# Two-layer hybrid block: attention's loads get an order of their own, other stages' weights are loaded ahead and split by GpSimd

## The chip, the cores and the metric

The kernel runs on one core of a Trainium2 chip. The metric is the device time of one execution in microseconds (us). The engines are TensorE (PE; its weight loads are listed apart as PEld), VectorE (DVE), ScalarE (ACT), GpSimd (POOL) and SyncE (SP), which in this kernel issues every transfer.

## The reference

The reference is a two-layer block with fp32 inputs and outputs: 1024 latent tokens (`x`) and 256 context tokens (`ctx`) of width 1024. Four mixers share one in-projection and one out-projection:

```
for l in range(2):
    sh, sc, gt = split(silu(c) @ w_mod[l] + b_mod[l], 3)       # the same from c_ctx for the context
    h  = rms_norm(x, g_pre[l]) * (1 + sc) + sh                 # latent and context
    p  = h @ w_in[l]
    a  = MLA attention, 4 heads (64 + 32 rotary), v 64         # softmax over 1024 + 256 keys
    g  = grouped-query attention, 4 heads, 2 key heads of 64   # the same keys' length
    s  = state-space mixer (two scans), finish: z = gelu(y + d*u); z * sigmoid(z @ glu_w + glu_b)
    y  = Hyena mixer (two long convolutions)
    x  = x + gt * rms_norm(concat[a, g, s, y] @ w_out[l], g_post[l])
```

The context is attended to and projected out in the first layer only. `a`, `g`, `s` and `y` are each multiplied by the silu of a part of `p`. `gt`, the gate, takes columns 2048 to 3071 of `w_mod`; `sh` and `sc` take the others.

## The kernel before

Everything is fp32. A large matmul takes three TensorE passes on operands split in two float32r parts, a rounded high one and the rest (names end in `h`/`hi` and `l`/`lo`); the split is a cast and a subtraction. Layer 0 runs from 0 to 1230 us, layer 1 from there to the end. In each layer come the mixers with the in-projection (`ipc`, operand `hh`, `hl`, weights `whi`, `wlo`), then attention, then the out-projection (`ops`).

**Attention** (`attention`, L1518 and below). The work is a list of units: for each pair of heads (g0, g1 of grouped-query attention, then m0, m1 of MLA), each block of 256 queries and each of the pair's two heads. Layer 0 has 40 units, layer 1 has 32, without the context's queries. A unit multiplies keys and queries for 1024 latent keys (`aS`) and 256 context keys (`acx`), takes the row maxima (`am`, DVE), the exponentials (`aP`, ACT), transposes them (`apt`), splits them (`aPh` on ACT, `aPl` on DVE) and multiplies by the values (`apo`). The sums' reciprocals are spread by GpSimd (`aLB`, L1665) and multiplied in. The string `ORDER` (L1515) writes the steps of neighbouring units out as one interleaved order, and a token (`keep`) makes the scheduler hold to it on every engine. Loads carry no token in this version: `load_q` asks for the queries `aq` three units ahead and, at a pair's first unit, for its keys `kst`, its values `vst` and, for m0, the rotary keys `krope`; the scheduler places them in SP's queue.

**Side work.** The last step of `ORDER`, `X`, calls `pump`, which advances a generator by one step a unit. In layer 0 it yields 24 steps of `mod_steps`: load 512 KB of `w_mod` (`mraw`), cast it on ACT (`mhi`, L326), subtract on GpSimd (`mlo`), multiply (`mps`, four matmuls a step), add to `msb`. Eight steps are this layer's gate, sixteen the next layer's shift and scale. Then, in both layers, 16 steps of `out_weights` load `w_out` (`owr`, 256 KB), cast it on ACT (`owh`, L1730) and subtract on GpSimd (`owl`). Layer 1's gate is not side work: `mod_plain` computes it right after the in-projection, ahead of attention, by 16 fp32 matmuls `mps<-wraw,csl`.

**The end of the mixers.** In layer 1 the last mixer work is `ssm_finish` (L1301): four chunks of 256 tokens, each with two loads `sgy`, `sgg` for each half, the gelu, which ends with `sz` on DVE, then `sglu` on PE, `sth` and a store to `mixD`. In layer 0 it is the Hyena mixer's context part, which ends with the stores `mixD<-hcz`.

**Order and queues.** The scheduler orders instructions by program order as far as their data and buffers allow. SP issues its transfers strictly in order and has eight semaphores, so a transfer also waits for the one eight before it to land. A buffer of a new pool that overlaps one of a closed pool waits for the last reader of that: `kst`, `vst` and `aq` of the first pair lie where the in-projection's operand was.

Of the kernel before, what the change touches and what calls it, by code (L numbers as in the profile page):

```python
# [11 lines left out]
F32 = mybir.dt.float32  # L12
# [175 lines left out]
class K:  # L188
# [114 lines left out]
    def mod_plain(self, l, blk):  # L303

        ps = self.f("mps")
        for k in range(8):
            raw = self.wp.tile([128, 512], F32, tag="wraw", name="wraw", bufs=2)
            self.load(raw, self.A["w_mod"][l, blk, :, k])
            self.mm(ps[:2], self.sc[:, k], raw, k == 0, k == 7)
        ms = self.wp.tile([4, 512], F32, tag="ipo", name="msb", bufs=3)  # L310
        self.nc.vector.memset(ms, 0.0)
        self.nc.scalar.copy(ms[:2], ps[:2])
        yield ms

    MODHI = "AA"

    def mod_steps(self, P, l, blk):
# [3 lines left out]
        for k in range(0, 8, 2):  # L321
            raw = P.tile([128, 2, 512], F32, tag="mraw", name="mraw", bufs=3)
            hi, lo = (P.tile([128, 2, 512], F32R, tag="m" + t, name="m" + t, bufs=2) for t in ("hi", "lo"))
            self.load(raw, self.A["w_mod"][l, blk, :, k:k + 2])
            for j, c in enumerate(self.MODHI):
                self.keep(nc.scalar.copy(hi[:, j], raw[:, j]) if c == "A" else (nc.gpsimd if c == "P" else nc.vector).tensor_copy(hi[:, j], raw[:, j]))  # L326
            self.lo(lo, raw, hi, nc.gpsimd)
            ps = self.f("mps")
# [36 lines left out]
    def mod_gates(self, l, steps):  # L365

        gD = self.mg = self.dram.tile([4, 1024], F32, name=f"modg{l}")
        for blk in range(2):
            for ms in steps(l, 4 + blk):
                if ms is not None:  # L370
                    self.store(gD[:, blk * 512:(blk + 1) * 512], ms)
                yield

    def mod_next(self, l, steps, P):

        *self.mod, put = self.mod_cols(l, P)
        for blk in range(4):
            for ms in steps(l, blk):
                if ms is not None:
                    put(blk, ms)  # L380
# [1137 lines left out]
    def attention(self, l, P, W, nq, side):  # L1518
# [18 lines left out]

        def keys(src):
# [435 lines left out]
```

## Time and profile before

| | us |
|---|---|
| median of 3 runs | 2233.22 (2231.14 to 2233.59) |
| profiled execution | 2229.03 |
| its span | 2226.9 |
| PE busy | 1956.9 (88%) |
| DVE busy | 1587.0 (71%) |
| ACT busy | 958.3 (43%) |
| POOL busy | 924.1 (41%) |
| chain that ended last | PE 43%, DVE 26%, DMA 12%, issue 6%, POOL 4%, ACT 4%, SPq 4% |

How to read it: the span is the first to the last instruction of the profiled execution. The chain follows the last instruction back to what released it, step by step; its DMA share is time in which the end of the kernel waited for a transfer, its SPq share for SP's queue. A timeline row gives start, length, engine, line, operation and tile, the number of instructions in a row, and in brackets idle time before it with its releaser. A windows row gives a stretch, its length, the busy time (and instructions) of PE, PEld, DVE, ACT and POOL (with a tile's name, those of its instructions, without the engines that have none), then the clock granted to TensorE (1.00 is 2.4 GHz), the busy share of the DMA engines and what they moved. A group row gives line, engine, operation, tiles, shape and count, then total busy us and mean ns, then idle time before and releasers. The trace can miss a few matmuls, so counts may be short by one or two.

### The profile page before, as it was taken

Reading aid. Unit: us, or ns where it says so; the run is one execution under the profiler, and the core shown is the slowest. Engines: PE = TensorE matmul, PEld = TensorE weight load, DVE = VectorE, ACT = ScalarE, POOL = GpSimd, SP = SyncE. Lnnn points to the kernel's source line nnn. Section 1 sums busy time; section 2 is a strip of 40 time slices with the busy share of each in tenths; the row PEclk is TensorE's granted clock in tenths of the full one; section 3 lists DMA queues with packets and bytes.
Section 4 is the critical chain, followed back from the end, with each engine's and each line's share of the span. In section 5 each row is a group of like instructions: output and inputs, shape, how many; then the busy total and the mean of one; then the engine's idle time right before and its main releaser. Section 6 shows DMA issues by size and latency. Waiting matters only on the chain.

```text
span 2226.9 us, 31563 instructions
## 1 busy us (share of the span) xinstructions
PE 1956.9 (88%) x10811; PEld 1624.3 (73%) x10811; DVE 1587.0 (71%) x2976; ACT 958.3 (43%) x2040; POOL 924.1 (41%) x726
## 2 busy tenths in 40 slices
PE   5797998889899689999799988987988968999888
PEld 2577887777778477778577776986766736899866
DVE  8799339856886479889444598399478836999822
ACT  4422233224333388777332322342232226987711
POOL 4656235664561133230156557247666602100034
PEclk8698899999999899999799987998999988999989
DMA  7323364337764845431343423363466577431063
GB/s 222 112 91 115 123 207 133 96 118 224 223 202 155 223 118 157 126 102 39 112 160 105 153 94 142 126 217 119 112 205 217 159 224 174 115 102 42 17 183 123
DMA packets 262402, 316.56 MB, mean 142 GB/s; under 512 B 46783, under 2 KB 203711, under 8 KB 258914
## 3 DMA queue, kind: packets, MB, share of 16 engines
q1 hardware_dynamic: 262242, 314.55, 46.4%
q8 instruction: 85, 1.39, 0.3%
q14 instruction: 75, 0.61, 0.1%
HBM read 207.61 MB, written 106.86 MB: 141 GB/s over the span
## 4 chain that ended last, share of the span: by engine, by line
PE 43%; DVE 26%; DMA 12%; issue 6%; POOL 4%; ACT 4%; SPq 4%; POOLq 0%; DVEq 0%; ACTq 0%
PE ipc L224 9%; PE ops L224 7%; PE apo L224 6%; PE apt L253 5%; PE aS L224 5%; SPq L201 4%; DVE sD L233 3%; DVE lU L233 2%; DMA px<-qkvD 2%; DVE sp L233 1%; PE acx L224 1%; PE lout L224 1%; ACT aPh L1637 1%; DMA krope<-mR 1%; PE hps L224 1%
## 5 line engine op out<-in xcount | busy, mean ns | idle before, releaser
L224 PE MATMUL ipc<-hh,whi 128*128 128x512 f32 (+2 forms) x992 | 386.8, 390 | 25.1 <-DVE ipt L236 10.1
L224 PE MATMUL ipc<-hl,whi 128*128 128x512 f32 (+2 forms) x992 | 380.6, 384 | 1.6 <-POOL hl L233 1.6
L224 PE MATMUL ipc<-hh,wlo 128*128 128x512 f32 (+2 forms) x992 | 381.7, 385 | 0.0
L233 DVE TENSOR_TENSOR aPl<-apt,aPh 128x512 fp32r<-128x512 f32 x328 | 224.8, 685 | 54.7 <-ACT aPh L1637 50.0
L224 PEld LDWEIGHTS ipc<-hh,whi 128*128 128x128 f32 x992 | 196.7, 198 | 60.9 <-DVE ipt L236 13.6
L233 POOL TENSOR_TENSOR wlo<-wraw,whi 128x512 fp32r<-128x512 f32 x108 | 158.8, 1475 | 147.1 <-ACT whi L443 145.7
L224 PEld LDWEIGHTS ipc<-hh,wlo 128*128 128x128 f32 x992 | 196.2, 198 | 32.4 <-issue 3.2
L1637 ACT CAST aPh<-apt 128x512 fp32r<-128x512 f32 x328 | 187.3, 592 | 71.5 <-PE apt L253 66.0
L224 PEld LDWEIGHTS ipc<-hl,whi 128*128 128x128 f32 x992 | 196.0, 198 | 30.1 <-POOL hl L233 2.3
L1665 POOL COPY aLB<-am 128x128 f32<-128x128 f32 x72 | 21.0, 292 | 419.5 <-DVE am L1657 419.5
L253 PE MATMUL apt<-ident,aP 128*128 128x128 f32 x1312 | 191.2, 276 | 2.5 <-DVE aPl L233 1.3
L1602 DVE TENSOR_REDUCE am<-aS 128x1 f32<-128x1024 f32 x128 | 155.8, 1217 | 33.6 <-PE aS L224 33.4
L224 PE MATMUL aS<-kst,aq 128*128 128x512 f32 x512 | 155.1, 426 | 21.7 <-DMA aq<-gP 12.2
L246 ACT ACTIVATE aP<-aS,am,rs 128x1024 f32<-128x1024 f32 x128 | 155.9, 1218 | 19.1 <-DVE am L243 17.4
L224 PE MATMUL apo<-aPh,vst 128*128 128x256 f32 x656 | 140.7, 312 | 23.7 <-ACT aPh L1637 18.6
L253 PEld LDWEIGHTS apt<-ident,aP 128*128 128x128 f32 x1312 | 150.3, 141 | 10.9 <-DVE aPl L233 5.5
L224 PE MATMUL apo<-aPl,vst 128*128 128x256 f32 x656 | 125.0, 288 | 3.4 <-DVE aPl L233 3.3
L224 PEld LDWEIGHTS apo<-aPh,vst 128*128 128x128 f32 x656 | 97.3, 192 | 39.1 <-ACT aPh L1637 24.7
L443 ACT CAST whi<-wraw 128x512 fp32r<-128x512 f32 x124 | 75.4, 618 | 99.0 <-PE ipc L224 52.4
L224 PEld LDWEIGHTS aS<-kst,aq 128*128 128x128 f32 x512 | 89.8, 196 | 36.6 <-issue 19.7
L224 PEld LDWEIGHTS apo<-aPl,vst 128*128 128x128 f32 x656 | 100.8, 191 | 11.4 <-DVE aPl L233 6.5
L224 PE MATMUL ops<-owh,omh 128*128 128x512 f32 x288 | 94.8, 410 | 15.7 <-ACT omh L1749 10.5
(372 smaller groups left out, 4469.6 us busy)
## 6 DMA issues: line engine op xcount, KB each, us to landing
wraw<-in_w_col_dram SPq DMA_DIRECT2D x64, 256.0 KB, 3.0
wraw<-in_w_mod_dram SPq DMA_DIRECT2D x48, 256.0 KB, 3.4
mraw<-in_w_mod_dram SPq DMA_DIRECT2D x24, 512.0 KB, 4.1
kst<-mK SPq DMA_DIRECT2D x16, 640.0 KB, 8.7
omx<-mixD SPq DMA_DIRECT2D x18, 512.0 KB
ogt<-gD SPq DMA_DIRECT2D x18, 512.0 KB, 4.3
k<-kt SPq DMA_DIRECT2D x16, 512.0 KB, 3.5
lk<-k SPq DMA_DIRECT2D x8, 1024.0 KB, 7.3
```

What stands on the lines that cost most here:

```text
L201: self.nc.sync.dma_start(out=out, in_=in_)
L224: self.keep(self.nc.tensor.matmul(out, lhsT, rhs, start=start, stop=stop))
L233: self.keep((eng or self.nc.vector).tensor_tensor(out=out, in0=a, in1=b, op=op))
L246: self.keep(self.nc.scalar.activation(out=out, in_=in_, func=func, **k))
L253: self.keep(self.nc.tensor.transpose(out, in_, self.ident[:p, :p]))
L443: self.nc.scalar.copy(hi, raw)
L1602: self.keep(nc.vector.tensor_reduce(out=x["m"][:, 2 + qi:3 + qi], in_=x["S"][qi], axis=AX.X, op=ALU.max))
L1637: self.keep(nc.scalar.copy(h, ps))
L1665: self.keep(nc.gpsimd.tensor_copy(x["LB"][:, :, o:o + 64], x["m"][:, 10:12].unsqueeze(2).to_broadcast([128, 2, 64])))
```

## The change

- `load` returns its instruction, and attention's own loads go through `fetch`, which stamps them with a second token: among themselves they keep the written order, and are not placed ahead of it.
- Attention takes three pools. The first pair's keys, values and all query buffers (`kst0`, `vst0`, `aq`) come from a pool above the in-projection's operand in memory, the later pairs' from another one.
- `feed` loads side work's weights ahead: `mraw` two steps ahead in three buffers, `owr` three ahead in four (two buffers before).
- The cast of `w_mod` and `w_out` to the high part moves from ACT to GpSimd, which does the subtraction as before: a 128x1024 `CAST` and a 128x1024 `TENSOR_TENSOR` for a step of `w_mod`.
- The products of a `mod_steps` step are put off to the next `pump` (`later`) and carry the attention token there; `pump` runs from unit 0 on.
- Layer 1's gate becomes eight `mod_steps` steps of its attention's side work; `mod_plain` goes.

```diff
-        self.nc.sync.dma_start(out=out, in_=in_)
+        return self.nc.sync.dma_start(out=out, in_=in_)
@@ -300,39 +300,49 @@
-    def mod_plain(self, l, blk):
...
-    def mod_steps(self, P, l, blk):
+    def feed(self, P, tag, shape, srcs, ahead):
+
+        queue, srcs = [], iter(srcs)
+
+        def more():
+            src = next(srcs, None)
+            if src is not None:
+                t = P.tile(shape, F32, tag=tag, name=tag, bufs=ahead + 1)
+                self.load(t, src)
+                queue.append(t)
+
+        for _ in range(ahead):
+            more()
+        while queue:
+            more()
+            yield queue.pop(0)
+
+    def mod_feed(self, P, blocks):
+
+        return self.feed(P, "mraw", [128, 2, 512],
+                         (self.A["w_mod"][l, b, :, k:k + 2] for l, b in blocks for k in range(0, 8, 2)), 2)
+
+    def mod_steps(self, P, feed, l, blk):
...
         for k in range(0, 8, 2):
-            raw = P.tile([128, 2, 512], F32, tag="mraw", name="mraw", bufs=3)
+            raw = next(feed)
             hi, lo = (P.tile([128, 2, 512], F32R, tag="m" + t, name="m" + t, bufs=2) for t in ("hi", "lo"))
-            self.load(raw, self.A["w_mod"][l, blk, :, k:k + 2])
-            for j, c in enumerate(self.MODHI):
-                self.keep(nc.scalar.copy(hi[:, j], raw[:, j]) if c == "A" else (nc.gpsimd if c == "P" else nc.vector).tensor_copy(hi[:, j], raw[:, j]))
+            nc.gpsimd.tensor_copy(hi, raw)
             self.lo(lo, raw, hi, nc.gpsimd)
-            ps = self.f("mps")
-            for j in range(2):
-                self.mm(ps[:4], self.sp[:, k + j], hi[:, j], j == 0, False)
-                self.mm(ps[:2], self.sp[:, k + j, 0:2], lo[:, j], False, j == 1)
-            if k == 0:
-                self.keep(nc.vector.tensor_copy(ms, ps[:4]))
-            else:
-                self.tt(ms, ps[:4], ms, ADD)
+
+            def products(k=k, hi=hi, lo=lo):
+                ps = self.f("mps")
+                for j in range(2):
+                    self.mm(ps[:4], self.sp[:, k + j], hi[:, j], j == 0, False)
+                    self.mm(ps[:2], self.sp[:, k + j, 0:2], lo[:, j], False, j == 1)
+                if k == 0:
+                    self.keep(nc.vector.tensor_copy(ms, ps[:4]))
+                else:
+                    self.tt(ms, ps[:4], ms, ADD)
+
+            self.later.append(products)
             yield ms if k == 6 else None
@@ -368,7 +378,7 @@
...
-                    self.store(gD[:, blk * 512:(blk + 1) * 512], ms)
+                    self.later.append(partial(self.store, gD[:, blk * 512:(blk + 1) * 512], ms))
...
@@ -1515,17 +1525,29 @@
...
-    def attention(self, l, P, W, nq, side):
+    def attention(self, l, pools, nq, side):
...
+        W, L, P = pools
...
+        self.later = []
+
         def pump():
+
+            late, self.later = self.later, []
+            for f in late:
+                f()
             self.token = None
-            next(side, None)
+            more = next(side, self)
             self.token = token
+            return more is not self or bool(self.later)
+
+        def fetch(dst, src):
+
+            self.tc.stamp_issue_order_token(self.load(dst, src).ins, f"ald{l}")
 
...
+        count = [0]
+
         def keys(src):
-            t = P.tile([128, 2, 1280], F32R, tag="kst", name="kst", bufs=4)
-            self.load(t[0:64], src)
-            self.load(t[64:128], src)
+            i = count[0] % 4
+            count[0] += 1
+            t = (L if i else P).tile([128, 2, 1280], F32R, tag=f"kst{i}", name="kst")
+            fetch(t[0:64], src)
+            fetch(t[64:128], src)
             return t
...
-            v = P.tile([128, 10, 2, 192], F32R, tag="vst", name="vst", bufs=2)
+            v = (L if p else P).tile([128, 10, 2, 192], F32R, tag=f"vst{p}", name="vst")
             if kind == "g":
                 k = keys(self.gP[2, p * 64:p * 64 + 64])
                 pr["k"] = [k, k]
-                self.load(v[:, :, 0, :], self.gV[:, :, p, :])
+                fetch(v[:, :, 0, :], self.gV[:, :, p, :])
...
-                    self.krope = P.tile([128, 1280], F32R, tag="krope", name="krope")
+                    self.krope = L.tile([128, 1280], F32R, tag="krope", name="krope")
...
-                q = pr["q"] = W.tile([128, 2, 2, 256], F32R, tag="aq", name="aq", bufs=3)
+                q = pr["q"] = P.tile([128, 2, 2, 256], F32R, tag="aq", name="aq", bufs=3)
...
@@ -1712,24 +1738,25 @@
             for f, off, latent in order:
                 if off is None:
-                    f()
+                    if i >= 0:
+                        f()
                 elif 0 <= i + off < n and (units[i + off]["lat"] or not latent):
                     f(units[i + off])
+        while pump():
+            pass
         self.token = None
...
-        for k in range(8):
-            for h in (slice(0, 512), slice(512, 1024)):
-                raw = R.tile([128, 512], F32, tag="owr", name="owr", bufs=2)
-                self.load(raw, self.A["w_out"][l, :, k, h])
-                self.nc.scalar.copy(wh[:, k, h], raw)
-                self.lo(wl[:, k, h], raw, wh[:, k, h], self.nc.gpsimd)
-                yield
+        halves = [(k, slice(h, h + 512)) for k in range(8) for h in (0, 512)]
+        feed = self.feed(R, "owr", [128, 512], (self.A["w_out"][l, :, k, h] for k, h in halves), 3)
+        for k, h in halves:
+            raw = next(feed)
+            self.nc.gpsimd.tensor_copy(wh[:, k, h], raw)
+            self.lo(wl[:, k, h], raw, wh[:, k, h], self.nc.gpsimd)
+            yield
...
-        if l:
-            for _ in k.mod_gates(l, k.mod_plain):
-                pass
...
         def side(R):
-            if l == 0:
-                with k.pool("ma", side="right") as M:
-                    steps = partial(k.mod_steps, M)
-                    yield from k.mod_gates(0, steps)
+            with k.pool("ma", side="right") as M:
+                gates, cols = [(l, 4), (l, 5)], [(1, b) for b in range(4)] if l == 0 else []
+                steps = partial(k.mod_steps, M, k.mod_feed(M, gates + cols))
+                yield from k.mod_gates(l, steps)
+                if cols:
                     yield from k.mod_next(1, steps, M)
             O = wo.enter_context(k.pool("wo", side="right"))
             yield from k.out_weights(l, O, R)
-        with k.pool("att") as W, k.pool("ast") as P:
-            k.attention(l, P, W, n, side(W))
+
+        with k.pool("att") as W, k.pool("asl") as L, k.pool("ast") as P:
+            k.attention(l, (W, L, P), n, side(W))
```

SP at the start of layer 0's attention (`gP`, `gV`: keys, queries, values in memory; `gD`: gate columns). Before:

```order
L201 DMA mixD_77<-hcz_5250 128x256
L201 DMA gD_78<-ipt 128x512
L201 DMA kst<-gP_4160 64x2560 x2
L201 DMA gD_78<-ipt 128x256
L201 DMA vst<-gV_4161 128x10x192
L201 DMA aq<-gP_4160 64x2x256 x5
L201 DMA mraw<-in_w_mod_dram 128x1024 x3
L201 DMA aq<-gP_4160 64x2x256
L201 DMA gpre<-in_g_pre_dram 128x8
```

After:

```order
L201 DMA mixD_77<-hcz_5250 128x256
L201 DMA kst<-gP_4160 64x2560 x2
L201 DMA vst<-gV_4161 128x10x192
L201 DMA aq<-gP_4160 64x2x256 x3
L201 DMA gD_78<-ipt 128x512
L201 DMA aq<-gP_4160 64x2x256 x3
L201 DMA gD_78<-ipt 128x256
L201 DMA owr<-in_w_out_dram 128x512 x4
L201 DMA mraw<-in_w_mod_dram 128x1024 x3
L201 DMA gpre<-in_g_pre_dram 128x8
```

The first keys, values and three query halves stand right behind `hcz` now, the second pair's keys and everything of MLA are no longer among these rows, and `owr` x4 comes ahead of `mraw`.

PE at the start of layer 1's attention (`sglu`: `ssm_finish`; `mps`: the gate). Before:

```order
L224 MATMUL sglu<-sz,sgw 128x256 x4
L224 MATMUL mps<-wraw,csl 2x512 x2
L224 MATMUL sglu<-sz,sgw 128x256 x2
L224 MATMUL mps<-wraw,csl 2x512
L224 MATMUL sglu<-sz,sgw 128x256 x2
L224 MATMUL mps<-wraw,csl 2x512 x4
L224 MATMUL aS<-kst,aq 128x512 x4
L224 MATMUL acx<-kst,aq 128x256 x4
```

After:

```order
L224 MATMUL sglu<-sz,sgw 128x256 x2
L224 MATMUL ipc<-hh,wlo 128x512
L224 MATMUL sglu<-sz,sgw 128x256 x4
L224 MATMUL aS<-kst,aq 128x512 x4
L224 MATMUL sglu<-sz,sgw 128x256 x8
L224 MATMUL acx<-kst,aq 128x256 x4
L224 MATMUL aS<-kst,aq 128x512 x8
```

The gate's matmuls are gone; the last eight `sglu` matmuls stand between the first unit's `aS` and its `acx`.

POOL at the start of layer 0's attention. Before:

```order
L233 TENSOR_TENSOR mlo<-mraw,mhi 128x1024 x3
L1665 COPY aLB<-am 128x2x64 x2
L233 TENSOR_TENSOR mlo<-mraw,mhi 128x1024 x3
L1665 COPY aLB<-am 128x2x64
L233 TENSOR_TENSOR mlo<-mraw,mhi 128x1024
L1665 COPY aLB<-am 128x2x64
L233 TENSOR_TENSOR mlo<-mraw,mhi 128x1024
```

After:

```order
L332 CAST mhi<-mraw 128x1024 x2
L233 TENSOR_TENSOR mlo<-mraw,mhi 128x1024
L1691 COPY aLB<-am 128x2x64
L233 TENSOR_TENSOR mlo<-mraw,mhi 128x1024
L1691 COPY aLB<-am 128x2x64
L332 CAST mhi<-mraw 128x1024
L233 TENSOR_TENSOR mlo<-mraw,mhi 128x1024
L1691 COPY aLB<-am 128x2x64
L332 CAST mhi<-mraw 128x1024
```

The casts stand in GpSimd's queue between the spreads `aLB`, one cast and one subtraction to a unit.

## Rows read from the trace of the kernel before

**Rows 1.** Chain that ended last, layer 0's attention start: start us, us, what.
```profile
766.90 15.31 DMA mraw<-in_w_mod_dram
```

**Rows 2.** TensorE timeline there: start, us, tile and count, [idle before <-releaser].
```profile
733.88 0.28 PE L224 MATMUL ipc<-hh,wlo 128*128 128x256 f32 x1
746.31 2.04 PE L224 MATMUL aS<-kst,aq 128*128 128x512 f32 x4 [12.15 <-DMA aq<-gP]
...
782.96 0.59 PE L224 MATMUL mps<-mhi,csp 128*4 128x512 f32 x1 [11.18 <-ACT mhi L326]
```

**Rows 3.** Timeline of SyncE's issues, same stretch.
```profile
725.37 2.58 SPq L201 DMA_DIRECT2D mixD<-hcz  x2
...
733.19 1.15 SPq L201 DMA_DIRECT2D kst<-gP  x2
...
756.11 9.53 SPq L201 DMA_DIRECT2D kst<-mK  x4
```

**Rows 4.** Windows: stretch, length, busy us (instructions) by engine, clock, DMA share, GB/s.
```profile
734.00:740.00 6.00, 0.16 (x2) 0.00 (x0) 0.42 (x1) 0.38 (x1) 0.00 (x0) 0.77 1.00 225
740.00:747.00 7.00, 0.69 (x2) 0.62 (x3) 0.00 (x0) 0.00 (x0) 0.00 (x0) 0.50 1.07 281
```

**Rows 5.** The same view, seven stretches inside the two attentions.
```profile
748.20:795.20 47.00, 32.88 (x188) 25.74 (x187) 29.26 (x49) 29.10 (x61) 15.10 (x9) 0.83 0.90 233
795.20:828.20 33.00, 32.46 (x225) 27.51 (x224) 31.20 (x58) 30.46 (x64) 10.74 (x8) 1.00 0.31 93
946.80:986.60 39.80, 36.66 (x245) 31.75 (x244) 33.17 (x56) 32.45 (x69) 17.72 (x17) 1.00 0.40 114
1021.00:1053.60 32.60, 32.60 (x238) 30.37 (x237) 30.41 (x55) 26.19 (x56) 1.18 (x4) 1.00 0.09 26
1839.60:1861.30 21.70, 20.46 (x116) 16.45 (x114) 17.84 (x30) 16.33 (x36) 0.58 (x2) 0.84 1.04 222
1861.30:1913.00 51.70, 42.01 (x268) 36.78 (x267) 38.07 (x69) 41.43 (x87) 21.76 (x21) 0.90 0.45 120
1920.20:1950.10 29.90, 29.90 (x215) 26.86 (x213) 29.24 (x55) 26.19 (x57) 1.17 (x4) 1.00 0.32 102
```

**Rows 6.** The same view, instructions of tile `acx` alone.
```profile
1839.60:1861.30 21.70, 2.84 (x13) 2.36 (x12) 2.04 (x3) 3.98 (x12) 0.84 1.04 222
1861.30:1913.00 51.70, 4.00 (x20) 3.17 (x21) 3.42 (x5) 6.58 (x20) 0.90 0.45 120
```

**Rows 7.** The same view, instructions of tile `mps` alone.
```profile
748.20:795.20 47.00, 6.10 (x20) 1.70 (x20) 2.71 (x4) 0.00 (x0) 0.83 0.90 233
795.20:828.20 33.00, 4.32 (x17) 1.36 (x16) 2.72 (x4) 0.00 (x0) 1.00 0.31 93
```

**Rows 8.** TensorE timeline at layer 1's attention start.
```profile
1793.99 0.39 PE L224 MATMUL ipc<-hh,wlo 128*128 128x512 f32 x1
...
1823.20 1.13 PE L224 MATMUL sglu<-sz,sgw 128*128 128x256 f32 x4
...
1839.57 1.05 PE L224 MATMUL acx<-kst,aq 128*128 128x256 f32 x4
```

**Rows 9.** VectorE timeline, same stretch, tile `sz` of the SSM's last stage.
```profile
1797.00 0.40 DVE L236 SCALAR_TENSOR_TENSOR sz<-sgg,sgy 128x256 f32<-128x256 f32 x1
...
1820.46 0.99 DVE L236 SCALAR_TENSOR_TENSOR sz<-sgg,sgy 128x256 f32<-128x256 f32 x2
```

**Rows 10.** GpSimd's groups, whole span; then durations of `wlo`, ns min/median/max.
```profile
L233 POOL TENSOR_TENSOR mlo<-mraw,mhi 128x1024 fp32r<-128x1024 f32 x24 | 57.2, 2384 | 105.5 <-ACT mhi L326 101.2 <-DMA mraw<-in_w_mod_dram 3.1 <-PE mps L224 1.1
...
L1665 POOL COPY aLB<-am 128x128 f32<-128x128 f32 x72 | 21.0, 292 | 419.5 <-DVE am L1657 419.5
...
L233 POOL TENSOR_TENSOR wlo<-wraw,whi x108: 1261/1340/3731, 9.4 to 1763.3; 128x512 fp32r<-128x512 f32 x108
```

**Rows 11.** VectorE's `am<-am` groups, 946.8 to 986.6, then 1021 to 1053.6.
```profile
L233 DVE TENSOR_TENSOR am<-am 128x2 f32<-128x2 f32 x4 | 3.8, 962 | 0.0
...
L233 DVE TENSOR_TENSOR am<-am 128x2 f32<-128x2 f32 x4 | 0.6, 150 | 0.0
```

More of the change, by code (lines that the diff above doesn't have):

```diff
@@ L301, in mod_block @@
         return ms
-    def mod_plain(self, l, blk):
-        ps = self.f("mps")
-        for k in range(8):
[L307 to L315, printed above, removed]
-    def mod_steps(self, P, l, blk):
+    def feed(self, P, tag, shape, srcs, ahead):
[15 more added lines that the diff above has]
+    def mod_steps(self, P, feed, l, blk):
         ms = P.tile([4, 512], F32, tag="msb", name="msb", bufs=2)
@@ L379, in mod_next @@
                 if ms is not None:
-                    put(blk, ms)
+                    self.later.append(partial(put, blk, ms))
                 yield
@@ L1553, in load_pair @@
                 if p == 0:
-                    self.krope = P.tile([128, 1280], F32R, tag="krope", name="krope")
+                    self.krope = L.tile([128, 1280], F32R, tag="krope", name="krope")
                     for s in range(4):
-                        self.load(self.krope[s * 32:s * 32 + 32], self.mR[:, s % 2])
+                        fetch(self.krope[s * 32:s * 32 + 32], self.mR[:, s % 2])
                 pr["k"] = [keys(self.mK[p, h * 64:h * 64 + 64]) for h in range(2)]
-                self.load(v, self.mV[:, :, 2 * p:2 * p + 2, :])
+                fetch(v, self.mV[:, :, 2 * p:2 * p + 2, :])
                 pr["v"] = [v[:, :, 0], v[:, :, 1]]
@@ L1567, in load_q @@
                 c = slice(x["q"] * 256, x["q"] * 256 + 256)
-                q = pr["q"] = W.tile([128, 2, 2, 256], F32R, tag="aq", name="aq", bufs=3)
+                q = pr["q"] = P.tile([128, 2, 2, 256], F32R, tag="aq", name="aq", bufs=3)
                 src = (self.gP if pr["kind"] == "g" else self.mQ)[p, :, :, c].rearrange("(h d) s n -> s d h n", h=2)
-                self.load(q[0:64, 0], src[0])
-                self.load(q[64:128, 0], src[1])
+                fetch(q[0:64, 0], src[0])
+                fetch(q[64:128, 0], src[1])
                 if pr["kind"] == "m":
@@ L1574, in load_q @@
                     for s in range(4):
-                        self.load(q[s * 32:s * 32 + 32, 1], src[s // 2])
+                        fetch(q[s * 32:s * 32 + 32, 1], src[s // 2])
             q, k = pr["q"], pr["k"][h]
@@ L1714, in attention @@
                 if off is None:
-                    f()
+                    if i >= 0:
+                        f()
                 elif 0 <= i + off < n and (units[i + off]["lat"] or not latent):
                     f(units[i + off])
+        while pump():
+            pass
         self.token = None
-        for _ in side:
-            pass
     def out_weights(self, l, P, R):
@@ L1725, in out_weights @@
         wl = P.tile([128, 8, 1024], F32R, name="owl")
-        for k in range(8):
-            for h in (slice(0, 512), slice(512, 1024)):
-                raw = R.tile([128, 512], F32, tag="owr", name="owr", bufs=2)
-                self.load(raw, self.A["w_out"][l, :, k, h])
-                self.nc.scalar.copy(wh[:, k, h], raw)
-                self.lo(wl[:, k, h], raw, wh[:, k, h], self.nc.gpsimd)
-                yield
+        halves = [(k, slice(h, h + 512)) for k in range(8) for h in (0, 512)]
[5 more added lines that the diff above has]
+            yield
         self.wo = wh, wl
@@ L1898, in dit_kernel @@
             k.inproj_gate(l, g, n, k.wp)
-        if l:
-            for _ in k.mod_gates(l, k.mod_plain):
-                pass
         px.close()
```

1 line of the change is left out of this document (removed).

## The prediction

> **What bounds the kernel now.** I read the busy shares first, then the chain of waits, then the timelines and windows of the places where the chain leaves TensorE. TensorE is busy for 88% of the span, so a gain must come from where it waits or stretches. Four such places touch the change.
>
> First, the start of layer 0's attention. The in-projection's last matmul starts at 733.88, and attention's first at 746.31, after 12.15 us of waiting for queries [rows 2]. SP issues the first keys at 733.19 only, though its queue before them was through at 725.37 + 2.58 = 727.95 [rows 3]: their buffers lie on the operand that the last matmuls read. From 734 to 747 the DMA engines are fully busy [rows 4].
>
> Second, a stall inside that attention. The chain has 15.31 us of an `mraw` transfer issued at 766.90 [rows 1], and TensorE waits 11.18 us, until 782.96, for the cast of that tile [rows 2]. The load was queued behind MLA's keys, whose four issues held SP for 9.53 us from 756.11 [rows 3], long before MLA's first unit.
>
> Third, ScalarE in the units that cast `w_out`: four units take 39.80 us against 32.60 for the same four without side work, and ScalarE has 32.45 busy instead of 26.19 [rows 5].
>
> Fourth, the start of layer 1's attention. The last in-projection matmul is at 1793.99, the last `sglu` at 1823.20, and the first `acx` at 1839.57 [rows 8]: 45 us for the SSM's last stage, the gate and the first keys' way. The first eight units after it take 21.70 + 51.70 = 73.40 us [rows 5]; the DVE counts of 3 and 5 in [rows 6], one a unit, give their number. They cast `w_out`, and run into late loads, while four undisturbed units of the same pair kind take 29.90, or 7.475 each [rows 5].
>
> **The change part by part.** The sum is made against the profiled execution, 2229.0; the median of the runs shown is 4.2 above it.
>
> *A. Layer 0's first keys.* They no longer wait for the operand. They can be issued behind the `hcz` stores at 727.95 instead of 733.19, 5.2 us earlier, and the first query halves stand ahead of the two gate stores and of `mraw`. What has to land before the first unit is two times 640 KB of keys, 960 KB of values and two query halves of 128 KB, 2.5 MB. At the 225 to 281 GB/s of [rows 4] that is 8.9 to 11.1 us, with one us for issues: first matmul at 738 to 740. The in-projection's last matmuls end at 734.2 and their loads of weights are through by then, so nothing else competes. I take 740, a gain of 6.3; bounds 4 (the old distance of 13.1 us from issue to matmul, and another us behind a store) and 8.5 (the 281 GB/s).
>
> The Trainium skill's page "DMA: Bandwidth & Descriptors", section "Measured (HBM→SBUF, 128 partitions, SWDGE, issued from GpSimd)", gives 341 GB/s for a transfer of 1 MB. By it the 2.5 MB would take 7.3 us and the first matmul stand near 737, 3 us more of gain. The trace has 225 and 281 with the DMA engines' share at 1.00 and above [rows 4], and I keep to these.
>
> *B. The stall after it.* The first four units take 47.00 us with 20 `mps` matmuls, five steps; the next four 33.00 with four steps (17 seen) [rows 7]. MLA's keys are gone from SP's queue here and `mraw` is two steps ahead. Four units with five steps at the undisturbed price are 33.00 plus one step, (33.00 − 29.90)/4 = 0.78: 33.8. Gain 13.2; bounds 5 (the units still start at a clock of 0.83 instead of 1.00, and `owr` now stands ahead of `mraw`) and 14. Steps done later cost the same 0.78 each.
>
> *C. ScalarE's casts of `w_out`, layer 0.* Four units go from 39.80 to 32.60: 7.2. Only if GpSimd hides them: its 17.72 busy in these units includes the subtractions that stay, so room is 22 us for some 13 casts. Bounds 3 and 9 (a fifth unit).
>
> *The price of a GpSimd cast* has no row. Below is the copy `aLB` of 128 elements in 0.292 us, so eight of these for 1024, 2.3 us. Above is the slowest subtraction of 512 elements, 3.731 us, twice, 7.5 [rows 10]. The median row, 1.340 for 512 with two inputs, gives 2.7. I take 2.4, that of `mlo` [rows 10], since a cast reads one input less. A unit with a step then has 2.4 + 2.4 + 0.3 = 5.1 us of GpSimd in 8.25: hidden. Behind a late GpSimd stands the next `aLB`, and behind a late `mlo` the products, which TensorE takes in strict order; being put off by a unit they have 8 us of room.
>
> *D. Layer 1's start.* The gate's 16 fp32 matmuls and their loads leave the gap, and keys wait for no operand. But `ssm_finish` stays: its last eight `sglu` stand on TensorE between the first `aS` and the first `acx`, so the attention waits for the last chunk. In the trace the first `sz` is at 1797.00 and the last at 1820.46 [rows 9], 23.5 us for three chunks further, and the last `sglu` ends 3.9 after that [rows 8]. The first chunk's loads now stand ahead of the Hyena store, and I put its `sz` at 1789, before the end of the in-projection. Then 1789 + 23.5 + 3.9 is 1816.4, and with 1.5 us for the `owr` and `mraw` loads that now stand ahead of the last chunk's, the first `acx` is at 1818. Gain 21.6. Bounds: 37 if the chunks, without `wraw` between their loads, run down with the in-projection (`acx` 8 us behind 1794), and 7.5 if the last chunk's loads wait for 1.5 MB of `mraw` and for layer 1's keys (`acx` at 1832).
>
> *E. Layer 1's first units.* The three at low clock stay 21.70; five at 7.475 are 37.4; saved 73.40 − 59.1 = 14.3. Added are eight steps at 0.78, 6.2. Net 8.1; bounds 2 and 12.
>
> *F. What is new.* MLA's first keys and values are now fetched amid the units, with `aq` and `mraw` behind them in SP. The old issue of four held SP 9.53 us [rows 3], while queries are asked for three units (25 us) ahead. For each layer between 0 and 9.5; I take 3, as the queue ahead mostly covers it: loss 6. The layer-1 mixers are scheduled anew, too; I count 0, bounds 10 either way, since no row says which.
>
> Sum: −6.3 − 13.2 − 7.2 − 21.6 − 8.1 + 6 = −50.4, so 2178.6, and on the median 2183.
>
> **The rivals.** (1) *Layer 1 waits for the transfers.* `sgg` of the last chunk stands behind `mraw` in SP: the 7.5 of D's bound, 14.1 less: 2197. For it: the eight-semaphore chain; against it: only three such loads. (2) *Layer 1 is not held*: D's 37, 15.4 more: 2167. Against it the eight `sglu` ahead of `acx`. (3) *The transfers are the bound at both starts*, since the DMA engines are full there [rows 4] and the bytes stay: A gives 0, B 5, D 7.5, the rest as above: −7.2 − 5 − 7.5 − 8.1 + 6 = −21.8, 2211.
>
> (4) *GpSimd holds VectorE.* The `am<-am` sum of two inputs in SBUF takes 0.962 us in the units where GpSimd subtracts `owl`, and 0.150 where it doesn't [rows 11]. If each of the 64 steps meets one, 64 × 0.81 = 52 us less the 8 paid already in ten units: 2183 + 44 = 2227, about no change. Against it: `aLB` waits for that very sum, so casts behind it start after the sum is done. The Trainium skill's page "GPSIMD Engine Reference", section "Key points", says that the engine shares its SBUF interfaces with VectorE and contends with its instructions of two SBUF inputs; the trace agrees, 0.962 against 0.150.
>
> (5) *Slower: GpSimd's queue becomes the bound.* Place: `aLB` and the products behind cast and subtraction. With 7.5 for a cast a unit needs 7.5 + 2.4 + 0.3 = 10.2 against 8.25, and 32 steps lose 62: 2183 + 62 = 2245. It decides from a cast of 5.6 us on, and turns the sum's sign from 7.2. Against it: no steady row of GpSimd is that slow.
>
> **How the numbers follow.** Forecast 0.58, (1) 0.15, (2) 0.10, (3) 0.08, (4) 0.03, (5) 0.06. The forecast's own range, from halves of the bounds of B, D and F, is 2170 to 2196. To hold 8 in 10 it must reach (1) and (2) with their spread and (3): 2158 to 2215. A measurement can tell about 0.2%, 4.5 us. The forecast and (1) to (3) are all faster, 0.91, less 0.03 for terms that fail together: 0.88. The same: (4) and a little, 0.05. Slower: (5) and a bad schedule of layer 1's mixers, 0.07.
>
> **What would show it.** A: first `aS` near 740, keys issued at 728. B: no idle time of 11 us before an `mps`, first `mps` in the fourth unit. C: layer 0's `w_out` units at 8.2 to 8.4 us, ScalarE without `owh`. The cast row of GpSimd at 2.4 us or less. D: `acx` at 1818, the in-projection's end unmoved, and the wait before it named `sz` or `sgg`, not `kst`. E: five units at 7.5 to 8.3. F: waits for `aq` or `kst<-mK` of a few us at the start of m0. The prediction is wrong if the wait for `mraw` comes back as one for `mlo`, if VectorE's `am<-am` stays near 1 us throughout, or if the layer-1 mixers' stage, 1236 to 1782, changes length by more than 10 us.

## The result and the profile after

The changed kernel took 2194.45 us (median of 4, 2193.80 to 2200.36) against 2233.40 of the kernel before; the ratio of the runs is 0.9837 (95% interval 0.9820 to 0.9854). The profiled execution took 2194.1 us, its span is 2192.3 instead of 2226.9, so that the two profiles differ by 34.6 us, and the medians by 39. The table divides the two spans at the same points of the program; a unit is counted from the start of its `acx`.

| part of the span, us | before | after | difference | forecast |
|---|---|---|---|---|
| to the end of layer 0's in-projection | 734.2 | 730.4 | −3.8 | |
| from there to the first `acx` | 14.0 | 9.1 | −4.9 | A −6.3 |
| units 0 to 3 | 47.0 | 29.5 | −17.5 | B, C, one F: |
| units 4 to 38, to the start of unit 39 | 281.5 | 287.5 | +6.0 | −17.4 for both |
| to the end of layer 1's in-projection | 717.7 | 718.3 | +0.6 | 0 |
| from there to layer 1's first `acx` | 45.2 | 37.6 | −7.6 | D −21.6 |
| units 40 to 50 | 95.6 | 87.7 | −7.9 | E, one F: −5.1 |
| units 51 to the end | 291.7 | 292.1 | +0.4 | 0 |

At the start of layer 0's attention the timelines of SyncE, then of TensorE, show the keys behind the `hcz` store and the shorter wait for the queries (start, length, tile and count, idle time before):

```profile
723.88 0.32 SPq L201 DMA_DIRECT2D mixD<-hcz  x1
724.31 1.14 SPq L201 DMA_DIRECT2D kst<-gP  x2
...
726.21 3.11 SPq L201 DMA_DIRECT2D aq<-gP  x3
...
739.00 1.37 SPq L201 DMA_DIRECT2D mraw<-in_w_mod_dram  x3
```

```profile
730.13 0.28 PE L224 MATMUL ipc<-hh,wlo 128*128 128x256 f32 x1
737.70 2.05 PE L224 MATMUL aS<-kst,aq 128*128 128x512 f32 x4 [7.28 <-DMA aq<-gP]
```

The first `aS` waits 7.28 us instead of 12.15 [rows 2]. No wait of TensorE for the cast of `mraw` follows.

The windows of units 0 to 3, of four units with a step, of units 53 to 56, which now hold eleven casts of `w_out` on GpSimd, and of units 40 to 42 (columns as in [rows 5]):

```profile
739.50:769.00 29.50, 28.42 (x171) 24.08 (x170) 25.88 (x45) 22.49 (x49) 11.07 (x9) 0.87 0.47 154
769.00:803.50 34.50, 33.47 (x226) 27.13 (x225) 31.09 (x58) 26.33 (x57) 14.89 (x12) 1.00 0.54 152
1915.90:1947.00 31.10, 31.10 (x223) 28.21 (x222) 30.18 (x56) 26.18 (x56) 19.94 (x26) 1.00 0.47 143
1812.50:1831.10 18.60, 16.82 (x113) 14.60 (x113) 16.95 (x31) 16.22 (x36) 0.58 (x2) 1.00 0.59 141
```

In the kernel before, units 53 to 56 had no side work:

```profile
1950.10:1981.10 31.00, 31.00 (x222) 28.16 (x221) 30.05 (x56) 26.62 (x57) 1.18 (x4) 1.00 0.35 86
```

The first row answers to 47.00 us at a clock of 0.83 [rows 5]. It is not like for like: units 0 to 3 held five steps before and hold one now (four `mps` matmuls make a step; the first stand in the fourth unit), so four steps moved into units 4 to 38. The second row is the bad news: 34.50 where 33.00 was forecast. The third and the row before the change show that the eleven casts cost these units nothing, 31.10 us against 31.00. The fourth answers to 21.70 us at a clock of 0.84 [rows 5]: these three units now run at 1.00. GpSimd's casts (groups in layer 0's attention) are cheaper than I took them:

```profile
L233 POOL TENSOR_TENSOR mlo<-mraw,mhi 128x1024 fp32r<-128x1024 f32 x24 | 57.2, 2387 | 1.5
L332 POOL CAST mhi<-mraw 128x1024 fp32r<-128x1024 f32 x24 | 25.0, 1041 | 77.0 <-PE mps L224 42.1 <-DMA mraw<-in_w_mod_dram 31.0 <-issue 2.5
...
L1757 POOL CAST owh<-owr 128x512 fp32r<-128x512 f32 x16 | 9.6, 611 | 16.8 <-DMA owr<-in_w_out_dram 16.8
```

That is 1.04 us for 1024 elements, against 2.4 in the sum. GpSimd waits for `mps` there, 42.1 us in all, and no wait of TensorE for GpSimd shows in units 0 to 24.

At layer 1's start the timelines of TensorE, then SyncE, show what holds it now:

```profile
1774.25 0.58 PE L224 MATMUL ipc<-hh,wlo 128*128 128x512 f32 x1
1780.19 3.75 PE L224 MATMUL sglu<-sz,sgw 128*128 128x256 f32 x8 [5.36 <-DVE sz L236]
1791.59 2.05 PE L224 MATMUL aS<-kst,aq 128*128 128x512 f32 x4 [7.65 <-DMA aq<-gP]
...
1808.98 3.51 PE L224 MATMUL sglu<-sz,sgw 128*128 128x256 f32 x8 [12.71 <-DVE sz L236]
1812.47 0.73 PE L224 MATMUL acx<-kst,aq 128*128 128x256 f32 x4
```

```profile
1773.24 0.38 SPq L201 DMA_DIRECT2D mixD<-hyt  x1
1773.73 1.35 SPq L201 DMA_DIRECT2D kst<-gP  x2
...
1788.26 3.18 SPq L201 DMA_DIRECT2D aq<-gP  x5
1791.54 0.54 SPq L201 DMA_DIRECT2D owr<-in_w_out_dram  x1
...
1793.12 1.38 SPq L201 DMA_DIRECT2D mraw<-in_w_mod_dram  x3
...
1797.76 0.56 SPq L201 DMA_DIRECT2D sgg<-uD  x1
```

TensorE waits 7.65 us for queries, and then 12.71 us for the last chunk's `sz`. The loads of that chunk, `sgg` at 1797.76, stand behind five query loads, four `owr` and three `mraw`. ScalarE's and VectorE's timelines of the same stretch show the chunks from the first `sz` to the last, and two waits between them:

```profile
1770.96 0.42 DVE L236 SCALAR_TENSOR_TENSOR sz<-sgg,sgy 128x256 f32<-128x256 f32 x1
...
1788.50 0.84 ACT L246 ACTIVATE sth<-sglu,sgb 128x256 f32<-128x256 f32 x2 [9.51 <-DMA mixD<-sth]
...
1804.79 2.25 DVE L236 SCALAR_TENSOR_TENSOR sgy<-sgg,sdd,sgy 128x256 f32<-128x256 f32 x2 [7.54 <-DMA sgg<-uD]
...
1808.51 0.99 DVE L236 SCALAR_TENSOR_TENSOR sz<-sgg,sgy 128x256 f32<-128x256 f32 x2
```

The three chunks behind the first take 37.6 us instead of the 23.5 of [rows 9]. ScalarE waits 9.51 us for a store that frees a buffer of `sth`, and VectorE 7.54 us for the last chunk's `sgg`. The keys were issued 54 us earlier than before (1827.92), the first `acx` came only 27 us earlier, and 20 of these were gained before the end of the in-projection.

### The profile page after: what moved, and what is told of

Same layout as the page of the kernel before. It is cut to its first block, busy times and chain, and to the rows that moved or that the text cites. A ratio compares the mean times of both kernels' runs of the same rounds, so it can differ in the third digit from the quotient of the medians.

```text
span 2192.3 us, 31534 instructions
## 1 busy us (share of the span) xinstructions
PE 1937.6 (88%) x10811; PEld 1617.4 (74%) x10811; DVE 1593.3 (73%) x2982; ACT 916.5 (42%) x1958; POOL 992.0 (45%) x798
## 4 chain that ended last, share of the span: by engine, by line
PE 44%; DVE 29%; DMA 10%; issue 6%; POOL 5%; SPq 3%; ACT 2%; POOLq 0%; DVEq 0%; ACTq 0%
PE ipc L224 8%; PE apo L224 7%; PE ops L224 6%; PE aS L224 6%; PE apt L253 6%; DVE lU L233 3%; DVE sD L233 3%; SPq L201 3%; PE acx L224 2%; DVE sp L233 1%; PE mps L224 1%; DMA aq<-gP 1%; DVE aPl L233 1%; DVE lX L233 1%; PE fdft L224 1%
## 5 line engine op out<-in xcount | busy, mean ns | idle before, releaser
L233 DVE TENSOR_TENSOR aPl<-apt,aPh 128x512 fp32r<-128x512 f32 x328 | 224.0, 684 | 20.9 <-ACT aPh L1663 17.0
L224 PE MATMUL aS<-kst,aq 128*128 128x512 f32 x512 | 153.7, 423 | 20.5 <-DMA aq<-gP 14.9
L224 PE MATMUL apo<-aPh,vst 128*128 128x256 f32 x656 | 138.2, 308 | 14.9 <-ACT aPh L1663 9.0
L224 PE MATMUL ops<-owh,omh 128*128 128x512 f32 x288 | 94.4, 408 | 19.4 <-ACT omh L1776 13.6
```

Of the source, the lines that this page charges most:

```text
L224: self.keep(self.nc.tensor.matmul(out, lhsT, rhs, start=start, stop=stop))
L233: self.keep((eng or self.nc.vector).tensor_tensor(out=out, in0=a, in1=b, op=op))
```

## The experiments

Each ratio below is to the kernel before, run beside that version; spans, distances and units are those of the profiled executions. A distance is the time from the end of layer 1's in-projection to its first `acx`.

**What holds layer 1's attention.** The theory: the loads of `ssm_finish` behind attention's and the weights' transfers. The rival: the volume of these.

```diff
# ssm_finish, layer 1: four buffers for sgy and sgg, the loads asked for first
+        first = {(c0, hf): loads(c0, hf) for c0 in range(0, N, 256) for hf in range(2)} if l else {}
```

> The changed kernel with one thing more: in layer 1, ssm_finish gets four buffers for sgy and sgg instead of two and asks for its chunks' loads first, so that the last chunk's loads stand ahead of most of attention's queries and of mraw and owr in SyncE's queue; keys and values stay where they are. Theory 1, the last chunk's loads are what holds layer 1's attention: last sz from 1809 to about 1790, the first acx from 1812.5 to 1794 to 1798, span 2174 to 2179 instead of 2192.3, ratio to before about 0.976. Theory 2, the transfers' volume holds it (keys, values, mraw and owr all have to pass): first acx within 4 us of 1812 and span 2188 to 2193, ratio 0.982 to 0.984.

Measured 2193.0 us, ratio 0.9833 (0.9813 to 0.9854), span 2191.4; from the in-projection's end to `acx` 34.0 us. The numbers are the second theory's, but the trace shows another reason for them. The loads came early, and the wait moved on: ScalarE's timeline there shows `sth` waiting for a buffer, which a store of an earlier chunk frees:

```profile
1791.97 0.47 ACT L246 ACTIVATE sth<-sglu,sgb 128x256 f32<-128x256 f32 x1 [9.27 <-DMA mixD<-sth]
...
1801.60 0.47 ACT L246 ACTIVATE sth<-sglu,sgb 128x256 f32<-128x256 f32 x1 [4.96 <-DMA mixD<-sth]
1805.46 0.47 ACT L246 ACTIVATE sth<-sglu,sgb 128x256 f32<-128x256 f32 x1 [3.38 <-DMA mixD<-sth]
```

These stores, too, stand in SyncE's queue among the attention's loads, and the 9.51 us of the changed kernel were such a wait. So both were mended, in layer 1:

```diff
-            ... name="sgy", bufs=2 / name="sgg", bufs=2 / name="sth", bufs=2
+            ... bufs=3 / bufs=3 / bufs=4, the loads asked for first
```

> The changed kernel with three buffers for sgy and sgg and four for sth in layer 1's ssm_finish, its loads asked for first: all its loads stand ahead of mraw and owr in SyncE's queue, and no tanh of a chunk waits for a store of the chunk before it (in e1_chunk_loads the loads were early, but ScalarE waited 9.3, 5.0 and 3.4 us for stores mixD<-sth to land and free sth). Theory 1, loads and stores of ssm_finish behind attention's and the weights' transfers are what holds the attention: distance from the in-projection's end to the first acx 18 to 26 us instead of 37.6, span 2178 to 2186. Theory 2, each small transfer behind the 2.5 MB of keys and values lands late wherever it stands: distance above 32 us, span 2188 to 2195.

2187.0 us, ratio 0.9801 (0.9781 to 0.9820), span 2186.6; the distance is 29.6 us, between the two. From the issue of the first keys to the first `acx` it is 29.0 us (1779.27 to 1808.24) against 38.7 in the changed kernel. All of the difference lies between the first `aS` and the first `acx`, 10.4 us instead of 20.9: that is what the chunks' loads and stores held. The stretch from the keys to `aS` stayed, 18.5 us against 17.9, and it is not the way of the keys themselves, whose second half landed at 1789.22. SyncE's timeline shows the second half of the first queries issued 15 us after the keys, behind loads and stores of the chunks; in the changed kernel it was 14.5 us (1788.26). `aS` starts 3 us after it in both:

```profile
1779.27 1.39 SPq L201 DMA_DIRECT2D kst<-gP  x2
...
1794.62 1.89 SPq L201 DMA_DIRECT2D aq<-gP  x3
```

No run puts these queries ahead of the chunks.

The other way round, `ssm_finish` ahead of the keys' preparation:

```diff
-LANES = "spfh", "hspf"
+LANES = "spfh", "hsfp"
```

> The changed kernel with LANES of layer 1 as hsfp instead of hspf: ssm_finish is issued ahead of prep (attention's queries, keys and values), and its loads and stores are long done when attention's first loads come. Theory 1, what holds layer 1's attention is ssm_finish's chain of loads and stores, which stands in SyncE's queue behind attention's loads and the weights: no sglu behind the first aS, from the end of the in-projection to the first acx 18 to 24 us instead of 37.6, span 2174 to 2182. Theory 2, whichever of the two comes last holds it: prep ends later by what ssm_finish took, the distance stays at 34 to 40 us and the span within 5 us of 2192.

2198.1 us, ratio 0.9865 (0.9844 to 0.9886), span 2195.4. The span is the second theory's, the distance neither's: 31.1 us, and the in-projection ends later, too (729.2 us from unit 39 to its end instead of 718.3). No `sglu` is left at the start, but the preparation now ends late, its stores stand ahead of the keys in the queue, and `aS` waits 24.53 us:

```profile
1792.62 2.64 SPq L201 DMA_DIRECT2D mK<-sp  x2
...
1798.57 1.15 SPq L201 DMA_DIRECT2D kst<-gP  x2
```

```profile
1813.91 2.04 PE L224 MATMUL aS<-kst,aq 128*128 128x512 f32 x4 [24.53 <-DMA aq<-gP]
```

**The place in memory and the order.** For the pools:

```diff
-        with k.pool("att") as W, k.pool("asl") as L, k.pool("ast") as P:
+        with k.pool("att") as W, k.pool("ast") as P, k.pool("asl") as L:
```

> The changed kernel with the pool of the first pair's keys, values and queries opened ahead of the one of the later pairs, so that it lies on the in-projection's operand again; the loads' order and all else stay. Theory 1, the place in memory gives the earlier start: layer 0's first aS from 737.7 to 744 to 747, layer 1's first keys behind the end of ssm_finish, its first acx 5 to 15 us later, span 2204 to 2216. Theory 2, the order of the loads gives it: span within 4 us of 2192.

2212.1 us, ratio 0.9915 (0.9888 to 0.9942), span 2212.4: the first theory, though each start came later than it had it. The wait for the first queries is back in layer 0, where the first `acx` comes 14.9 us after the in-projection instead of 9.1, and in layer 1 the keys were issued at 1815.04 only and the distance is 48.4 us (TensorE's timeline of both starts):

```profile
749.97 2.05 PE L224 MATMUL aS<-kst,aq 128*128 128x512 f32 x4 [13.05 <-DMA aq<-gP]
...
1830.72 2.05 PE L224 MATMUL aS<-kst,aq 128*128 128x512 f32 x4 [17.17 <-DMA aq<-gP]
```

For the token on the loads:

```diff
-            self.tc.stamp_issue_order_token(self.load(dst, src).ins, f"ald{l}")
+            self.load(dst, src)
```

> The changed kernel without the token on attention's loads (the pools, the loads ahead and GpSimd's casts stay): MLA's keys and the second pair's keys and values go back to the start of SyncE's queue, ahead of mraw. Theory 1, the order of the loads is what takes the 11 us wait for mraw away: a wait of 5 to 12 us comes back for mraw in units 1 to 4 of layer 0, some in layer 1, span 2198 to 2210. Theory 2, loading two steps ahead and the products put off by a unit are enough: span within 3 us of 2192.

2197.8 us, ratio 0.9853 (0.9834 to 0.9872), span 2196.4. The wait returned, but as one for the subtraction, and only 3.33 us long; units 0 to 3 took 32.2 us:

```profile
766.55 0.59 PE L224 MATMUL mps<-mlo,csp 128*2 128x512 f32 x1 [3.33 <-POOL mlo L233]
```

By the spans the token is worth 4 us, less than expected and not resolved: the intervals of the two ratios overlap. The products put off by a unit might have hidden the rest, so they were put back into the step itself, with and without the token on the loads:

```diff
-            self.later.append(products)
+            products()
```

> The changed kernel with the products of a w_mod step issued in the step itself, without the attention's token, and not put off to the next pump; the loads' order, the pools and GpSimd's casts stay. Theory 1, the loads' order alone took the 11 us wait for mraw away: layer 0's first four units at 28 to 31 us as in the changed kernel (29.5), before it 47.0. Theory 2, it needs the products to be late, since TensorE stands in order behind cast and subtraction: a wait of 3 to 8 us for mlo in units 2 to 4, first four units at 33 to 38 us. Beside that the scheduler may place mps better than the token does: units with a step at 8.25 to 8.4 instead of 8.63.

> As e10_at_once and, as in e3_no_load_order, without the token on attention's loads: MLA's keys stand ahead of mraw in SyncE's queue again, and the products are not put off. Theory 1, the loads' order is what matters: first four units at 38 to 48 us, as before the change. Theory 2, the products put off are what matters and e10 already shows it: the first four units within 3 us of e10's.

With the token (e10) 2174.2 us, 0.9765 (0.9748 to 0.9781), units 0 to 3 at 30.2: the loads' order alone takes the wait away. Without it (e12) 2189.9 us, 0.9832 (0.9812 to 0.9851), units 0 to 3 at 40.4, and TensorE waits for the cast again:

```profile
761.21 0.59 PE L224 MATMUL mps<-mhi,csp 128*4 128x512 f32 x1 [5.59 <-POOL mhi L332]
```

So either the order or the products' delay would nearly do. Units 0 to 3 hold three steps in e10 and e12, one in e3 and in the changed kernel, so that the order without the delay does even a little better than these times say. The delay with the token costs: units 0 to 38, which hold all 24 steps in each version, take 306.2 us in e10 instead of 317.0, and units with a step 8.1 and 8.4. The rest of its 20 us comes from layer 1's mixers, which were scheduled anew: up to the end of the in-projection they take 9.5 us less, and the distance is 27.5. Some is lost again: units 51 to the end take 297.8 us instead of 292.1. The timelines of GpSimd and TensorE show where:

```profile
1889.59 0.61 POOL L1757 CAST owh<-owr 128x512 fp32r<-128x512 f32 x1 [8.12 <-DMA owr<-in_w_out_dram]
...
1897.09 0.69 PE L253 MATMUL alb<-ident,aLB 128*128 128x128 f32 x2 [4.51 <-POOL aLB L1691]
```

GpSimd's casts, too, can hold the attention: here GpSimd waited 8.12 us for `owr` to land, with `aLB` behind it, and TensorE stood idle for 4.51 us.

**The price of a step.** VectorE's timeline of a unit with a step in the changed kernel:

```profile
769.41 0.68 DVE L233 TENSOR_TENSOR aPl<-apt,aPh 128x512 fp32r<-128x512 f32 x1
770.63 0.68 DVE L233 TENSOR_TENSOR msb<-mps,msb 4x512 f32<-4x512 f32 x1 [0.54 <-PE mps L224]
771.24 0.67 DVE L1625 TENSOR_REDUCE am<-acx 128x2 f32<-128x512 f32 x1
```

`msb`, the add of the products, stands ahead of the maximum of `acx`, and waits for `mps`, which TensorE takes behind `acx`. The next unit's exponentials hang on that maximum. In `ORDER`, `C+2` is that `acx`, `L4` the split `aPl` of the unit's last block, and `X` the call of `pump`. First `mps` went ahead of `acx`:

```diff
-             ... "Vl2 C+2 L4 X"
+             ... "Vl2 X C+2 L4"
```

> The changed kernel with the step X of ORDER moved ahead of C+2, so that the deferred products (mps) stand ahead of the next unit's acx on TensorE, and not behind it, in front of the transposes. Theory 1, a step costs 1.15 us instead of the forecast 0.78 because VectorE waits for mps (0.54 us) before the maximum of acx: the units with a step go from 8.63 to about 8.27, 32 steps by 0.37, span about 2180, ratio 0.979. Theory 2, the step's price is its own 0.93 us of TensorE wherever it stands: units at 8.5 to 8.7, span within 3 us of 2192.

2186.1 us, ratio 0.9801 (0.9771 to 0.9830), span 2182.6: the span is as the first theory had it, for another reason. Units with a step got dearer, 8.64 and 8.97 us for 8.41 and 8.85, since the add now stands ahead of the split `aPl`, which it delays. The gain is at layer 1's start: the scheduler ordered its mixers anew, the distance there is 18.1 us. Then the two halves apart, the add behind `L4`:

```diff
+             ... "Vl2 X C+2 L4 Y"    # X: mps; Y: the add, then the next step
```

> The changed kernel with mps ahead of the next unit's acx on TensorE (as in e2_mps_before_acx) and VectorE's add of its result behind the split of the unit's last block (behind L4), so that VectorE waits for mps at no place. Theory 1, a step's price is VectorE's wait for mps: units with a step 8.25 to 8.35 instead of 8.63, units 4 to 39 at 280 to 283 us instead of 287.5. Theory 2, the price is TensorE's 0.93 of mps: 8.4 or more, units 4 to 39 at 285 or more. As in e2 the schedule of layer 1's mixers moves with it, so the span is read by its parts.

2171.1 us, ratio 0.9746 (0.9726 to 0.9765), span 2169.3; units 4 to 38 at 278.5 us. The first theory. The add waits no more, and four units take 33.10 us instead of 34.50:

```profile
778.88 0.69 DVE L233 TENSOR_TENSOR aPl<-apt,aPh 128x512 fp32r<-128x512 f32 x1
779.54 0.68 DVE L233 TENSOR_TENSOR msb<-mps,msb 4x512 f32<-4x512 f32 x1
780.15 0.67 DVE L1636 TENSOR_REDUCE am<-acx 128x2 f32<-128x512 f32 x1
```

```profile
762.80:795.90 33.10, 33.10 (x230) 28.27 (x229) 32.21 (x59) 26.07 (x56) 14.94 (x13) 1.00 0.55 158
```

Of the 23 us of span, the cheaper step explains 8.8 in units 0 to 38 and 2.5 in units 40 to 50. Most of the rest is layer 1's start, where the distance is 18.3 us and the mixers, again scheduled anew, take 5 us more.

**The casts' engine.**

```diff
-            nc.gpsimd.tensor_copy(hi, raw)
+            for j in range(2):
+                nc.scalar.copy(hi[:, j], raw[:, j])     # and owh likewise
```

> The changed kernel with the casts of w_mod and w_out back on ScalarE; the subtractions stay on GpSimd, the loads ahead and the products put off by a unit stay too. Theory 1, ScalarE's casts lengthened the units: the units with w_out go from 8.1 back to 9 to 10, and layer 0's attention from 317 to 322 to 326 us, span 2197 to 2204. Theory 2, it was the lateness of the loads, not the engine of the cast: span within 3 us of 2192.

2215.9 us, ratio 0.9943 (0.9924 to 0.9962), span 2209.8, worse than the first theory had it: by the spans 17.5 us, of which 5.8 in units 4 to 38 and 13.6 in units 51 to 70. The profiled execution was the fastest of the four; by the ratios it is some 24 us. ScalarE's timeline in layer 1 shows why:

```profile
1912.73 0.60 ACT L1664 CAST aPh<-apt 128x512 fp32r<-128x512 f32 x1
1920.21 0.62 ACT L1758 CAST owh<-owr 128x512 fp32r<-128x512 f32 x1 [6.88 <-DMA owr<-in_w_out_dram]
1921.06 0.62 ACT L1758 CAST owh<-owr 128x512 fp32r<-128x512 f32 x1 [0.23 <-DMA owr<-in_w_out_dram]
1921.58 0.58 ACT L1664 CAST aPh<-apt 128x512 fp32r<-128x512 f32 x1
```

ScalarE takes its work in order: while it waits 6.88 us for the tile of one cast, the splits and exponentials behind that cast wait as well.

**The gate of layer 1**, computed ahead of attention as before:

```diff
+        if l:
+            for _ in k.mod_gates(l, k.mod_plain): ...
```

> The changed kernel with layer 1's gate computed where it was before the change, by 16 fp32 matmuls right after the in-projection, and not as eight steps amid layer 1's attention. Theory 1, the gate belonged to what held the attention back: the first acx comes 5 to 10 us later, the units get 8 steps by 1.15 = 9 us shorter, span within 3 us of 2192. Theory 2, with ssm_finish holding the attention the gate's matmuls find 37 us of an idle TensorE: first acx at 1812 to 1815, units 40 to 50 at 78 to 80 us instead of 87.7, span 2182 to 2186.

2190.9 us, ratio 0.9834 (0.9814 to 0.9855), span 2189.1. The first `acx` is at 1812.6, as the second theory had it, but units 40 to 50 take 85.0 us, not 79: twelve of the matmuls had slipped into units 40 and 41. By the spans it is 3 us, which the intervals don't resolve: no effect of the gate's place shows.

**Both mends together** (`ssm_finish` as in e9, the add as in e8):

> e8_add_split and e9_loads_stores together. If theory 1 of both holds, units with a step stay at 8.1 to 8.4 us and the distance from the in-projection's end to the first acx at 18 us or less, span 2162 to 2170; the schedule of e8 already has the last chunk's loads ahead of the weights, so that little more may come: then 2167 to 2172, the same as e8_add_split.

2169.4 us, ratio 0.9732 (0.9709 to 0.9756), span 2167.8: the best of all, though not to be told from e8. Its distance at layer 1's start is 16.4 us.

**What each part is worth.** Taken back alone, the place in memory costs 17 us by the ratios and 20 by the spans (e4), the casts' engine 24 and 18 (e7), the token on the loads about 4 (e3) and the gate nothing that can be told (e6); e3's and e6's intervals overlap with that of the changed kernel.

## Why the prediction held, and where it missed

The time lies in the range and in the forecast's own narrower one, near its upper end, and the gain was 39 us instead of 50, 34.6 by the profiles. The mechanisms of A, B and C held; two terms failed, the price of a step by 12 us and D by 14. That the time is still in the narrower range is in part luck: the 6 us of F did not come, and layer 1's first units ran at full clock, which gave 3. Without these two it would have been near 2204, outside it. Part by part:

- **A**: right in mechanism; e4 shows that the place in memory gives it. The distance fell by 4.9. The other 3.8 us by which the first `acx` came earlier are no gain: in the 14 profiles TensorE, VectorE and SyncE have the same order up to there, and the in-projection's end lies anywhere from 727.9 to 738.0.
- **B**: right. The wait of 11.18 us is gone. Units 0 to 3 fell by 17.5 us, but they hold four steps fewer, which at 0.78 each are 3.1; 14.4 are left for the forecast 13.2. The low clock is not gone with the wait: it is 0.87 over these units, for 0.83 before. The forecast credited the loads' order, with loading ahead, with all; e3, e10 and e12 show that order and delay each cover for the other.
- **C**: right in mechanism: eleven casts cost units 53 to 56 nothing on GpSimd, and e7 adds 5.8 us in layer 0 without them. Its 7.2 us were not measured alone, but the sum of layer 0 closes with them: B and C, −20.4, and 24 steps dearer by 0.37, +8.9, give −11.5, and units 0 to 38 fell by 11.6. I missed that the casts also keep ScalarE's queue free of waits for a landing, which e7 prices at 13.6 us in layer 1.
- **The price of a step** failed. "Steps done later cost the same 0.78 each" took the price from the order before, where `mps` stood ahead of `acx` and the add behind the split. With the attention's token on both it is (34.50 − 29.90)/4 = 1.15 us. For 32 steps the difference is 12 us, 8.9 of it in layer 0. With the add behind the split it is (33.10 − 29.90)/4 = 0.80, and units 0 to 38 take 308.2 us in e8 instead of 317.0, 8.8 less; in e10, without the delay, 306.2.
- **D** is the largest miss: 7.6 instead of 21.6. The step that failed is "with 1.5 us for the `owr` and `mraw` loads that now stand ahead of the last chunk's, the first `acx` is at 1818". The first chunk's `sz` came 3.9 us before the in-projection's end, where the sum has 5, and the last `sz` 4.0 before `acx`, where it has 3.9; but the 23.5 + 1.5 us for the three chunks between them were 37.6. Rival (1), with its bound of 7.5, is what happened, by the mechanism it named, the wait of 7.54 us for `sgg`, and by a second one, the wait of 9.51 us for a store that frees `sth`. Taking both away (e9) gave back 8 of the 14 us; behind the rest stand the queries issued late, which no run isolates. I had carried the chunks' pace over from a trace in which the keys and values were issued only after the chunks.
- **E**: 7.9 measured for 8.1, but by two errors that cancel: the eight steps are dearer by 3.1, and the first three units, for which the sum said "the three at low clock stay 21.70", take 18.60 at a clock of 1.00. No run shows why the clock was high there.
- **F**: not seen. Layer 0's first two MLA units take 16.7 us, before 17.6, layer 1's take 16.3 in both, and no wait for MLA's keys shows.

Rival (3) is refuted by A and B, (5) by the cast's 1.04 us, and (4) too: in the units with a step the sum `am<-am` takes 0.150 us (VectorE's group, 1840 to 1874). GpSimd's subtraction for a step is through there before the sum starts. Where a subtraction of `owl` runs at the same time the sum is still held: the second group (966 to 985) is two sums, of 0.149 and 1.200 us. But of the 64 sums only two are that long now, this one and one of 1.089 at 1913.

```profile
L233 DVE TENSOR_TENSOR am<-am 128x2 f32<-128x2 f32 x4 | 0.6, 150 | 0.0
...
L233 DVE TENSOR_TENSOR am<-am 128x2 f32<-128x2 f32 x2 | 1.3, 674 | 0.0
```

What stays open: why the mixers of layer 1 end 10 us earlier against the in-projection in e2, e8 and b2 (keys issued 10 us before its end instead of 1 us). The scheduler gave another order there, and by the distances of 16 to 18 us it is worth more than e9's change; no run isolates it.

## What to carry to other kernels

Work that is moved into a gap of another stage joins that stage's queues: before pricing it, list what stands ahead of the loads and of the stores which free buffers in the same in-order queue. When side work is given a fixed place in a hand-written order, put each half where its engine would not wait; an add that waited 0.54 us ahead of the critical maximum raised the price of a step from 0.80 to 1.15 us. Do not let a conversion of data that may land late stand in the queue of an engine on the critical path. Give it to one with room, and look at what shares its queue: on ScalarE such casts cost 17 us or more, and on GpSimd they cost nothing in the changed kernel, but 4.51 us once in e10, where `aLB` stood behind them.

## What was not expected of the hardware

GpSimd's cast with one input takes 1.041 us for 128x1024 and 0.611 for 128x512, no more than ScalarE's 0.619 for the latter, while its subtraction with two inputs takes 2.387 for 128x1024. And the same instruction order on TensorE, VectorE and SyncE gave ends 10 us apart at 730 us of the span, in profiles of 14 kernels, so a stage is best compared from the nearest common point.
